# One encoder layer in fp32 on one core: the instructions are ordered on a simulated timeline instead of a plain machine model

## The chip, the cores and the metric

The kernel runs on one core of one Trainium2 chip. Its time is the device time of one execution in microseconds. Before the change it is 2390.23 us, the median of three runs that lie between 2390.2 and 2392.87 us.

The core has five engines that each work through their own list of instructions in the order in which the program holds them: PE (TensorE, matrix products and transposes), DVE (VectorE), ACT (ScalarE), POOL (GpSimd) and SP (SyncE, which here does nothing but start transfers). An instruction waits on semaphores for its inputs and for the buffer it writes, and everything behind it on the same engine waits too. Transfers are started by SP, ACT or POOL instructions and then run on their own.

## The reference

One layer on 1024 tokens of width 1024, batch 1, all in float32. The three sub-layers are normed before and after:

```python
f = swiglu(rmsnorm(h, pre1), w_gate1, w_up1, w_down1);   h = h + 0.5 * rmsnorm(f, post1)     # width 2816
z = rmsnorm(h, pre2) @ w_in                                                                   # 1024 -> 3456
y_att  = attention(z[:, :1536])    # 8 heads of 64, rotary; three dilated windows (128,1), (512,4), (2048,16),
                                   # mixed by their softmax denominators; each head normed
y_rwkv = rwkv7(z[:, 1536:])        # 8 heads of 64, token shift, forward and backward delta-rule scans, summed,
                                   # group norm, bonus, gate
mix = concat(y_att, y_rwkv) @ w_out;                     h = h + rmsnorm(mix, post2)
f = swiglu(rmsnorm(h, pre3), w_gate2, w_up2, w_down2);   out = h + 0.5 * rmsnorm(f, post3)
```

## The kernel before

**Products.** Every large product splits its fp32 operands into a high part that PE takes in one pass and the remainder (`split`: ACT copies the high part, line 186, DVE subtracts it, line 187), and sums three matmuls: high by high, high by low, low by high. The two feed-forward parts use a recursion with seven products in place of eight (lines 81 and 415).

**The run, in order.** First feed-forward part (to about 690 us in the profiled execution); low-rank projections and attention values; projection of queries and keys with rotation (`project_attention`: products `zq` line 440, transposes `zt` line 486, copy `zts` line 488, stores to DRAM `q_d` and `kt_d` line 489; then one stream of RWKV columns, `zs`, lines 306 to 309); attention; RWKV; the out projection; the second feed-forward part.

**Attention** (`attention`, line 739). For each of eight heads a "far" part (scores `s`, line 626, row maximum, exponential, transposes line 638, values line 644, a trip through DRAM) and a "near" part of eight query tiles (scores lines 685 and 686, masked maximum on DVE line 687, exponential on ACT line 691, transposes line 700, values line 707); line 732 is DVE's product that closes a head. The far part and the operand copies of the next head (lines 660 to 665) are issued inside the near part of this one.

**The RWKV projection** (`project_rwkv`). Eleven column blocks of 128 in six groups; each block takes 48 matmuls of 128x512 (`zr`, line 510, 528 in all), fed by loads `zraw` on SP and splits `zh`, `zl`. DVE then mixes neighbouring tokens into `us` (lines 524, 525). Value blocks are reversed (line 605) and transposed (`vt`, line 611, 64 transposes).

**The scan** runs in chunks of 64 tokens, two per block, eight blocks, both directions at once. For each block n, `prep` loads decays and keys (`th_w`, `th_a`, `in`; the last has one buffer), builds the scaled operands on DVE (lines 808 to 822), multiplies them on PE (line 830) and masks the result into `lm` (line 832, DVE, eight of them); the diagonal pieces of `lm` go to DRAM (`d_x`, line 846). `solve` loads them back as `X` (through `load`, line 182), and inverts on DVE in 31 dependent steps of two instructions each (lines 866 and 868), closing with line 870; the result goes to DRAM again (lines 872, 873). `merge` takes it from there (lines 883 to 900), and `chain` runs two dependent steps per block (xu, st, y: lines 937 to 952), each of which hands the state on through line 968 on DVE. `project_attended` (transposes `yq` 1075, products `po` 1064, fed by `yat` 1072 and `yal` 1078) puts the attention half of the out projection between them. `finish_unit` (f_y line 994 and f_k line 997 on POOL, line 999 on DVE) turns the scan's output into operands of the out projection.

**What sets the order.** The Python program emits every instruction once, in the order of its calls, and a scheduler then makes the list of each engine. It may put an instruction anywhere that its data allow. Its ties go by the order of emission, which `high_priority()` around one piece at the start raises, and `issue_after` in `_GateUp.rest` (line 162) holds four sums behind a given store. The scheduler advances a machine model as it places instructions; in this kernel it is the plain one, the default of the context that line 1431 opens. Buffers, their number and their place in memory come from the pools and are the same in both versions, as are all lines of code.

## Time and profile before

| | |
|---|---|
| time, median of 3 runs | 2390.23 us (2390.2 to 2392.87) |
| profiled execution: its own time | 2398.21 us |
| its span, first to last instruction | 2396.4 us |
| mean granted TensorE clock | 0.951 |
| PE busy | 2233.1 us, 93% of the span |
| DVE, ACT, POOL busy | 1778.9, 1030.6 and 572.8 us |

Times in the trace count from the start of the span. Where the stages lie there: first feed-forward part 0 to 690; projections 690 to 914; attention 918 to 1170 (its first scores start at 918.22, line 732 of the last head at 1169.4); RWKV preps, solves, merges and chain 1170 to 1624; out projection 1634 to 1740; second feed-forward part to the end. A row of a timeline gives start, duration, engine, line, operation, output and inputs, shape, and in brackets the idle time of the engine before it with what ended it. A matmul's duration is longer than its share of PE, since matmuls overlap: what a matmul costs is the distance from its start to that of the next.

### The profile page before, as it was taken

To read this page: it belongs to the slowest core of one execution; us is meant where nothing else is said; L and a number is where in the kernel's file an instruction comes from. 1 tells how busy PE (TensorE), PEld (TensorE's weight loads), DVE (VectorE), ACT (ScalarE), POOL (GpSimd) and SP (SyncE) were. 2 spreads that over 40 slices of the span, in tenths; PEclk is the share of its full clock that TensorE was granted. 3 is DMA by queue.
4 is the path that set the end of the run, shared out by engine and by line. 5 is a ranking of instruction groups with operands and counts; after the bars stand their busy time and mean duration, and the time that the engine had idled before them with its cause. 6 is when DMAs were issued, how large, how long until landed. Compare 5 with 4: busy or idle time off the path is not lost. (4 is left out here: it accounts for less than half of the span.)

```text
span 2396.4 us, 39330 instructions
## 1 busy us (share of the span) xinstructions
PE 2233.1 (93%) x14532; PEld 1801.5 (75%) x14532; DVE 1778.9 (74%) x2917; ACT 1030.6 (43%) x1918; POOL 572.8 (24%) x668
## 2 busy tenths in 40 slices
PE   6999999999999998999986788898989999999997
PEld 4788888788786676778775577775768888887886
DVE  8899999865675345666556766746889999997565
ACT  4422333354676304556544444445442233335452
POOL 6244344500000010111101121132234443442000
PEclk8999999999999998999995698789989999999999
DMA  5344544576743415322366766558534544448655
GB/s 155 110 172 150 171 158 156 181 257 194 227 152 133 161 50 157 84 71 72 91 173 174 177 157 166 146 173 268 186 107 172 180 150 167 164 152 268 194 189 180
DMA packets 359763, 386.03 MB, mean 161 GB/s; under 512 B 73618, under 2 KB 268050, under 8 KB 359572
## 3 DMA queue, kind: packets, MB, share of 16 engines
q1 hardware_dynamic: 311968, 284.82, 39.5%
q0 software_dynamic: 27248, 86.05, 9.7%
q10 hardware_dynamic: 20356, 12.66, 1.8%
q8 instruction: 114, 1.87, 0.3%
q14 instruction: 77, 0.63, 0.1%
HBM read 257.53 MB, written 125.89 MB: 160 GB/s over the span
## 5 line engine op out<-in xcount | busy, mean ns | idle before, releaser
L186 ACT ACTIVATE wh<-raw 128x512 fp32r<-128x512 f32 (+1 forms) x273 | 168.2, 627 | 261.8 <-DVE raw L62 94.0
L81 PE MATMUL gu<-xh,wh 128*128 128x512 f32 x704 | 277.2, 394 | 2.3 <-ACT wh L186 1.1
L187 DVE TENSOR_TENSOR wl<-raw,wh 128x512 fp32r<-128x512 f32 (+1 forms) x273 | 275.6, 1013 | 2.1 <-ACT wh L186 1.2
L81 PE MATMUL gu<-xh,wl 128*128 128x512 f32 x704 | 275.9, 392 | 0.0
L81 PE MATMUL gu<-xl,wh 128*128 128x512 f32 x704 | 275.7, 392 | 0.0
L415 PE MATMUL pd<-gl,gwh 128*128 128x512 f32 x616 | 240.5, 390 | 2.5 <-DVE gl L187 2.5
L415 PE MATMUL pd<-gh,gwh 128*128 128x512 f32 x616 | 239.6, 390 | 0.6 <-DVE row L86 0.6
L415 PE MATMUL pd<-gh,gwl 128*128 128x512 f32 x616 | 239.8, 389 | 0.0
L86 DVE TENSOR_TENSOR row<-gu,row 128x512 f32<-128x512 f32 x308 | 206.3, 682 | 26.1 <-PE gu L81 24.2
L187 DVE TENSOR_TENSOR gwl<-graw,gwh 128x512 fp32r<-128x512 f32 (+1 forms) x176 | 117.9, 672 | 128.4 <-ACT gwh L186 125.7
L116 POOL DMA_DIRECT2D d_hid<-row x154 | 84.7, 551 | 473.3 <-DVE row L114 446.2
L186 ACT ACTIVATE gwh<-graw 128x512 fp32r<-128x512 f32 (+1 forms) x176 | 101.4, 576 | 188.4 <-PE pd L415 157.5
L81 PEld LDWEIGHTS gu<-xh,wh 128*128 128x128 f32 x704 | 133.5, 190 | 31.6 <-ACT xh L186 2.0
L81 PEld LDWEIGHTS gu<-xl,wh 128*128 128x128 f32 x704 | 133.4, 189 | 27.5
L81 PEld LDWEIGHTS gu<-xh,wl 128*128 128x128 f32 x704 | 133.1, 189 | 27.6
L415 PEld LDWEIGHTS pd<-gl,gwh 128*128 128x128 f32 x616 | 115.6, 188 | 28.0 <-DVE gl L187 4.3
L415 PEld LDWEIGHTS pd<-gh,gwh 128*128 128x128 f32 x616 | 115.6, 188 | 25.3 <-DVE row L86 1.0
L415 PEld LDWEIGHTS pd<-gh,gwl 128*128 128x128 f32 x616 | 115.7, 188 | 23.8
L187 DVE TENSOR_TENSOR gl<-raw,gh 128x512 fp32r<-128x512 f32 x160 | 112.3, 713 | 17.0 <-ACT gh L186 16.7
L94 ACT ACTIVATE row<-row 128x512 f32<-128x512 f32 x44 | 27.8, 633 | 221.3 <-DVE row L86 217.5
L145 POOL TENSOR_TENSOR ws<-ws 128x512 f32<-128x512 f32 x88 | 114.2, 1298 | 1.1
L186 ACT ACTIVATE gh<-raw 128x512 fp32r<-128x512 f32 x160 | 98.0, 621 | 33.7 <-DMA raw<-in_ffn_w_down_dram 21.8
(354 smaller groups left out, 5345.7 us busy)
## 6 DMA issues: line engine op xcount, KB each, us to landing
d_hid<-row POOLq DMA_DIRECT2D x154, 256.0 KB, 2.4
graw<-d_hid SPq DMA_DIRECT2D x132, 256.0 KB, 3.0
raw<-in_ffn_w_gate_dram SPq DMA_DIRECT2D x88, 256.0 KB, 3.0
raw<-in_ffn_w_up_dram SPq DMA_DIRECT2D x88, 256.0 KB, 3.3
ws<-in_ffn_w_down_dram SPq DMA_DIRECT2D x88, 256.0 KB, 4.5
d_ws<-ws POOLq DMA_DIRECT2D x88, 256.0 KB, 2.3
raw<-d_ws SPq DMA_DIRECT2D x88, 256.0 KB, 2.7
raw<-in_ffn_w_down_dram SPq DMA_DIRECT2D x66, 256.0 KB, 3.6
```

The lines of the kernel that those rows point to most:

```text
L81: self.K.nc.tensor.matmul(ps, a[:, k, :], b[:, k, :], start=(k == 0 and i == 0), stop=(k == 3 and i == 2))
L86: add = lambda o, x: V.tensor_tensor(o, ps, x, op=OP.add)
L94: A.activation(y[:, 0], y[:, 0], AF.Silu)
L116: put = lambda n, y: G.dma_start(self.hid[n - 1, j // 2], y)
L145: G.tensor_tensor(o, a, b, op=OP.subtract)
L186: self.nc.scalar.activation(h, src, AF.Copy)
L187: (eng or self.nc.vector).tensor_tensor(l, src, h, op=OP.subtract)
L415: T.matmul(ps[x], a[:, ts], b, start=(m == 0 and k == 0), stop=(m == NM - 1 and k == 2))
```

## The change

```diff
-    with tile.TileContext(nc) as tc:
+    with tile.TileContext(nc, schedule_with_timeline_sim=True) as tc:
```

The scheduler now advances a simulated timeline in which every engine and every transfer queue has its own occupancy, and chooses the next instruction of an engine by it. Nothing else differs: both programs hold the same instructions, lines, tiles and buffers, and the same number on each engine. What differs is the order of each engine's list, and with it where waits stand.

On PE, rows 481 to 2900 and 9139 to the end of 11544 instructions, which are the bodies of the two feed-forward parts, stand in the same order; on DVE, ACT, POOL and SP neighbours there change places by one to four. Rows 3850 to 8200, which hold attention, the RWKV projection and the scan, move by up to 1412 places. Three places follow.

PE, the end of the projections and the start of attention. `zs` are the last matmuls of the projection, `zt` the transposes of rotated queries, `s` the far scores of head 0, `pt` its transposes, `zr` the RWKV projection. Before:

```order
L306 MATMUL zs<-xh_5434,wh 128x512
L307 MATMUL zs<-xl_5435,wh 128x512
L309 MATMUL zs<-xh_5432,wl 128x512
L309 MATMUL zs<-xh_5434,wl 128x512
L626 MATMUL s_7793<-kp,qp 64x64 x16
L510 MATMUL zr<-xh_5432,zh 128x512
L638 MATMUL pt_7817<-ident,sb_7811 128x128 x4
L510 MATMUL zr<-xl_5433,zh 128x512
L510 MATMUL zr<-xh_5434,zh 128x512
```

Now:

```order
L309 MATMUL zs<-xh_5432,wl 128x512
L309 MATMUL zs<-xh_5434,wl 128x512
L486 MATMUL zt<-ident,zo 128x128 x12
L626 MATMUL s_7793<-kp,qp 64x64 x16
L510 MATMUL zr<-xh_5432,zh 128x512
L510 MATMUL zr<-xl_5433,zh 128x512
L510 MATMUL zr<-xh_5434,zh 128x512
L510 MATMUL zr<-xl_5435,zh 128x512
L510 MATMUL zr<-xh_5432,zl 128x512
L510 MATMUL zr<-xh_5432,zh 128x512
```

The transposes of the last three query tiles, three times four, now stand behind all `zs`; before, the last of them stood among the `zs`. Behind the scores stood one `zr` matmul ahead of `pt`, now stand 15. Over the whole of attention, from the first `s` to the last `po` of line 707, the list now holds all 528 `zr` and all 64 `vt` in place of 238 `zr` and no `vt`: 133, 99, 83, 107, 101 and 5 `zr` in heads 0 to 5 and none in the last two.

PE, the end of attention (`po` of line 707 is the last head's product with the values). Before:

```order
L510 MATMUL zr<-xh_5434,zl 128x512
L510 MATMUL zr<-xh_5434,zh 128x512
L707 MATMUL po<-vn,e_10134 64x64 x6
L510 MATMUL zr<-xl_5435,zh 128x512
L510 MATMUL zr<-xh_5434,zl 128x512
L510 MATMUL zr<-xh_5432,zh 128x512
L510 MATMUL zr<-xl_5433,zh 128x512
```

Now (`yq` and `po` of line 1064 are the attended projection, `lp` is prep's product):

```order
L707 MATMUL po<-vn,e_10090 64x64 x10
L707 MATMUL po<-vn,e_10117 64x64 x8
L700 MATMUL pt_10135<-ident,sb 128x128 x3
L707 MATMUL po<-vn,e_10134 64x64 x6
L1075 MATMUL yq<-ident,yat 128x128 x4
L830 MATMUL lp<-pr,bk 128x128 x12
L1064 MATMUL po<-woh,yah 128x512
L1064 MATMUL po<-wol,yah 128x512
L1064 MATMUL po<-woh,yal 128x512
```

Before, 290 `zr` and the 64 `vt` followed; now the preps follow at once, and the attended projections stand between them.

DVE, the start of solve 3 (`X` is the piece of `lm` that comes back from DRAM, 128x31 the first step of a solve). Before, from the closing row of solve 2:

```order
L821 TENSOR_TENSOR th_a<-th_a,in_12997 128x512
L868 TENSOR_TENSOR Ti<-Ti,ttmp 128x3x15
L822 TENSOR_TENSOR bk<-th_a,th_w 128x8x64
L866 TENSOR_TENSOR ttmp<-X,Ti 128x30
L1078 TENSOR_TENSOR yal<-yq,yah 128x512
L868 TENSOR_TENSOR Ti<-Ti,ttmp 128x2x15
L866 TENSOR_TENSOR ttmp<-X,Ti 128x16
L868 TENSOR_TENSOR Ti<-Ti,ttmp 128x16
L870 COPY X<-Ti 128x512
L1072 TENSOR_TENSOR yat<-yat,rs 128x512
L866 TENSOR_TENSOR ttmp<-X,Ti 128x31
L868 TENSOR_TENSOR Ti<-Ti,ttmp 128x31
```

Its own prep's last `lm` stands 23 rows ahead of the first step. Now:

```order
L832 TENSOR_TENSOR lm<-lp,k_tri 128x512 x2
L815 SCALAR_TENSOR_TENSOR bk<-bk,th_w 128x8x64
L822 TENSOR_TENSOR bk<-th_a,th_w 128x8x64
L832 TENSOR_TENSOR lm<-lp,k_tri 128x512 x2
L814 SCALAR_TENSOR_TENSOR bk<-th_a,in_12997 128x8x64
L815 SCALAR_TENSOR_TENSOR bk<-bk,th_w 128x8x64
L821 TENSOR_TENSOR th_a<-th_a,in_12997 128x512
L822 TENSOR_TENSOR bk<-th_a,th_w 128x8x64
L832 TENSOR_TENSOR lm<-lp,k_tri 128x512 x4
L866 TENSOR_TENSOR ttmp<-X,Ti 128x31
L868 TENSOR_TENSOR Ti<-Ti,ttmp 128x31
L866 TENSOR_TENSOR ttmp<-X,Ti 128x30
```

The last four `lm` of prep 3 stand directly ahead of the first step of solve 3. The number of DVE rows between the last `lm` of a block and the first step of its solve was 8, 19, 38, 23, 7, 16, 37 and 29 for blocks 0 to 7, and is 11, 13, 63, 0, 0, 5, 13 and 9. Solves 0 and 1, which stood apart, now alternate step by step.

After the last head DVE's list loses seven pairs of lines 524 and 525, nine of line 187, four of line 605 and eight of line 1055, which now stand inside attention. At the end of the scan one pair of line 999 now stands ahead of the third last chain step's line 968 and two more pairs ahead of the second last; before, the first line 999 came behind the second last chain step. At the program's start, up to about 80 us, DVE's splits of the first weights stand ahead of splits of the input that stood before them.

## The prediction, made before the changed kernel was run

> **What bounds the kernel now.** I read the page's busy line and slices first, then busy time by stage.
>
> ```profile
> span 2396.4 us, 39330 instructions
> PE   6999999999999998999986788898989999999997
> DVE  8899999865675345666556766746889999997565
> ```
>
> PE is full in every slice of the two feed-forward parts (up to slice 11 and from slice 29). Their PE list is the same in both programs, so 80 to 690 us and most of what follows 1760 can move only through neighbours that change places on DVE. The gaps lie in slices 15 and 20 to 26, and stages show them:
>
> ```profile
> 80.00:690.00 610.00, 607.11 (x2692) 500.52 (x2691) 518.92 (x637) 239.51 (x428) 179.57 (x209) 1.00 0.55 182
> 918.00:1170.00 252.00, 243.16 (x2433) 194.54 (x2434) 170.94 (x488) 154.45 (x341) 31.79 (x31) 0.94 0.31 89
> 1170.00:1313.00 143.00, 117.08 (x856) 97.06 (x854) 77.97 (x157) 62.97 (x115) 19.13 (x32) 0.82 0.62 163
> 1313.00:1624.00 311.00, 264.04 (x4181) 214.05 (x4180) 205.73 (x621) 141.62 (x266) 62.05 (x92) 0.84 0.63 166
> ```
>
> The columns are busy PE, weight loads, DVE, ACT, POOL, then granted clock, DMA share and GB/s. In the first row PE is busy 607 of 610 us. In the last two neither PE nor DVE (206 of 311 us) is full: a chain of short steps sets the time there, prep on DVE, store and load of `X`, solve on DVE, merge, chain step. The end of that chain (1624 us) lets the rest of the program begin, so the time moves by as much as it moves. I therefore follow four dates: the first scores of attention, its last head, the last solve, the last chain step.
>
> **The start of attention: +11 us.**
>
> ```profile
> 902.65 0.39 PE L440 MATMUL zq<-z0l,xh 128*128 128x512 f32 x1
> 902.88 0.39 PE L440 MATMUL zq<-z0h,xl 128*128 128x512 f32 x1
> 906.15 0.63 PE L486 MATMUL zt<-ident,zo 128*128 128x128 f32 x4 [0.16 <-DVE zo L482]
> 906.81 0.69 DVE L488 COPY zts<-zt 128x512 f32<-128x512 f32 x1 [0.81 <-PE zt L486]
> 907.81 0.75 POOL L489 DMA_DIRECT2D d_q<-zts  x1 [5.19 <-DVE zts L488]
> 914.34 0.62 PE L309 MATMUL zs<-xh,wl 128*128 128x512 f32 x2
> 918.22 3.39 PE L626 MATMUL s<-kp,qp 64*64 64x64 f32 x32 [3.26 <-DMA kp<-d_kt]
> ```
>
> Two starts of 128x512 matmuls lie 0.23 us apart; that is their price. The last `zt` starts at 906.15, and 12.1 us later, after copy, store and load, the scores start. In the new list three groups of `zt` stand behind all `zs`, whose last start is at 914.34 + 0.23 us. The first of the three can run then; if DVE is up to date so can the last, and the scores come at about 927; if not, each of the three waits for three DVE products and a copy of 0.69 us (2.8 us), up to 8 us in all, and they come at 935. I take 929, because DVE's list brings these products forward: +11 (8 to 17).
>
> **Attention: +45 us.** The stage by heads, `zr` alone, and DVE's closing product:
>
> ```profile
> L732 DVE TENSOR_TENSOR ya<-po,c x8: 684/684/692, 968.1 to 1169.4; 128x512 f32<-128x512 f32 x8
> 918.22:968.06 49.84, 11.34 (x30) 0.83 0.44 136
> 968.06:1153.44 185.38, 65.96 (x202) 0.96 0.29 80
> 1169.42:1257.00 87.58, 70.79 (x290) 0.98 0.57 155
> ```
>
> Attention lasts 918.2 to 1169.4, 251 us, with 240 `zr` (30, 202 and 8). 290 follow, and all of them move in: 290 x 0.227 = 66 us of PE, and 64 `vt` at 0.63/4 = 0.16 or less, at most 10; I count 7. Were nothing of it hidden, attention would last 251 + 73 = 324. What can hide it: six heads take 185.4 us with 202 `zr` (46 us), so a head without them takes about 23 us; head 0 takes 49.8 with 30 (7 us), 20 us more than such a head, in which PE waits for loads and splits. Head 0 now has 133 `zr`, which can fill those 20. In heads 1 to 4 (83 to 107 each, 19 to 24 us) some 5 us a head of gaps can be filled, by the granted clock of 0.96 and by the 14 us that the bare last head takes. That gives 324 - 40 = 284 at best. But they stand in blocks of 15 to 24, and each of those (3.4 to 5.4 us) holds up whichever `pt` or score behind it is ready, and a block waits itself for its splits on ACT and DVE. I take two thirds filled, 296: +45 (33 to 73). The last head then ends at 929 + 296 = 1225.
>
> **After attention: less work and fewer waits, -59 us.**
>
> ```profile
> L524 DVE SCALAR_TENSOR_TENSOR us<-u,c_rwkv_mu_prev,us 128x1023 f32<-128x1023 f32 x7 | 9.2, 1313 | 14.5 <-ACT us L523 14.5
> L525 DVE SCALAR_TENSOR_TENSOR us<-u,c_rwkv_mu_next,us 128x1023 f32<-128x1023 f32 x7 | 9.0, 1279 | 0.0
> L1055 DVE SCALAR_TENSOR_TENSOR wol<-wor,c_attn_out_g,woh 128x512 fp32r<-128x512 f32 x8 | 6.0, 744 | 0.0
> L187 DVE TENSOR_TENSOR zl<-zraw,zh 128x256 fp32r<-128x256 f32 x9 | 3.6, 424 | 5.5 <-ACT zh L186 5.5
> L605 DVE COPY vrev<-us 128x1024 f32<-128x1024 f32 x4 | 2.7, 686 | 0.0
> DVE pr L810 <- DMA in<-d_rk: 17.8, 5, 8.3
> ```
>
> These groups of 1170 to 1624 move into attention: 9.2 + 9.0 + 6.0 + 3.6 + 2.7 = 30.5 us of DVE. With them go their waits, 14.5 + 5.5, and the 8.3 us for which the first prep waited on keys that the projection had only just stored: 28.3. In attention they cost DVE nothing on the path while it is busy 171 of 252 us; if that cover went, their 30.5 us would return. `zr` itself was PE work beside these.
>
> **The solves: +27 us.** This is the term that decides.
>
> ```profile
> 1227.47 3.75 SPq L846 DMA_DIRECT2D d_x<-lm  x4
> 1237.76 1.11 SPq L182 DMA_DIRECT2D X<-d_x  x2
> 1244.95 0.18 DVE L866 TENSOR_TENSOR ttmp<-X,Ti 128x31 f32<-128x31 f32 x1
> 1364.00:1379.90 15.90, 8.29 (x26) 0.68 0.85 211
> sum 144.40, DVE 87.78; mean DVE 10.97
> L870 DVE COPY X<-Ti x8: 582/598/623, 1267.5 to 1584.0; 128x512 f32<-128x512 f32 x8
> ```
>
> From the first store of `d_x` to the first step of its solve it takes 17.5 us for block 0, 15.9 for block 3, the shortest of the eight. Summed over the eight blocks (windows from each store to its solve's start, of which one row and the sum are shown) that is 144.4 us; DVE worked in 87.8 of them and stood for 56.6. In the new list the instructions that stand there are 11, 13, 63, 0, 0, 5, 13 and 9; by the durations of their groups they hold 6, 4, 15, 0, 0, 3, 3 and 2 us, 33 in all. DVE is in order, so nothing from further down can fill in. With windows of 15.9 us DVE would stand 8 x 15.9 - 33 = 94 us, 38 more than now. If the load of `X` followed its store with nothing between on SP, a window could shrink to 3.75 us of issue and the median landings of both, which the next rows give:
>
> ```profile
> d_x<-lm SPq DMA_DIRECT2D x32, 64.0 KB, 3.7
> X<-d_x SPq DMA_DIRECT2D x16, 256.0 KB, 5.1
> ```
>
> 12.6 us, and 101 - 33 = 68, 11 more than now. In the new list SP does issue `X` right behind `d_x` in most blocks, so I take windows of 14.5: 116 - 33 = 83, +27 (11 to 38). The Trainium skill (DMA: Bandwidth & Descriptors, "Anatomy of one DMA") gives a DMA of the GpSimd path about 2 us plus its bytes over 436 GB/s; two in a row would take some 5 us, and by that estimate the new order would leave DVE standing some 19 us and this term would be about -37. The 17.5 us above do not bear it out here.
>
> The last solve, now ending with the row at 1584.0, comes at 1584 + 11 + 45 - 59 + 27 = 1608.
>
> **The end of the chain: +2 us; the start: +1.**
>
> ```profile
> 1593.65 1.39 DVE L968 TENSOR_TENSOR sv<-st,gc 64x512 f32<-64x512 f32 x2 [5.83 <-PE st L937]
> 1606.64 0.88 DVE L999 SCALAR_TENSOR_TENSOR f_k<-f_k,rkc,f_r 128x256 f32<-128x256 f32 x2 [11.60 <-POOL f_k L997]
> 1615.45 1.41 DVE L968 TENSOR_TENSOR sv<-st,gc 64x512 f32<-64x512 f32 x2 [2.81 <-PE st L937]
> PE pt L330 <- DVE xl L187: 17.7, 6, 10.1
> ```
>
> Line 999 waits 11.6 us for POOL, which waits for loads of the scan's output. Today two chain steps stand ahead of it; in the new list it stands ahead of them, so they are queued behind that wait and PE's next step behind them. But the last step cannot come before merge 7, 31 us after the last solve (1584 to 1615), and that covers it unless the wait exceeds some 20 us: +2 (0 to 15). In the first 80 us PE waits 17.7 us for DVE's splits, the same number of splits in another order: +1 (0 to 5). Swaps of neighbours in the feed-forward bodies: 0, hidden by PE at 607 of 610 us.
>
> **The sum.** 11 + 45 - 59 + 27 + 2 + 1 = +27 us. The profiled execution took 2398.21 us, 1.8 more than its span and 8.0 more than the median of the runs; it would become 2425, and the median 2390.2 + 27 = 2417.
>
> **Rivals.**
>
> *Attention swallows the projection (faster, 2380).* The `zr` fill all 40 us of gaps (+33) and the start costs its least (+8), the `X` windows shrink to 12.6 (+11): 8 + 33 - 59 + 11 = -7, and -10 with an attention a little closer to full. For it: today's 252 us hold many short gaps. Against: the blocks, and two last heads with no filler. It decides where attention ends before about 1205. Chance 0.24.
>
> *Loads in SP's list hold up attention (slower, 2450).* SP now issues twenty `zraw` loads ahead of the far load of head 0, and later groups of four between the loads of the next heads; each waits for a buffer of four, and what stands behind it on SP waits too. From its load (issued 915.98 us) to its first use a block took 7.8 us; if each of the last five of seven groups stalls a head so, +39 on the sum, less what the gaps give: about 2450. For it: SP is in order. Against: groups of `zraw` stood among the same loads before, in other numbers. Chance 0.14.
>
> ```profile
> 915.98 2.22 SPq L182 DMA_DIRECT2D zraw<-in_w_in_dram  x4
> 923.82 0.80 PE L510 MATMUL zr<-xh,zh 128*128 128x512 f32 x1 [2.21 <-ACT zh L186]
> ```
>
> *It cancels (2390).* Less work after attention pays for the longer attention and the windows: attention at +35, windows at +11, the start at +8 give -3 to +3. For it: the PE work is the same in sum. Chance 0.12.
>
> **How the numbers follow.** Forecast 0.50, rivals 0.24, 0.14 and 0.12. A change under 0.2% (4.8 us) cannot be told from none here. Faster by more: 0.24; within: 0.12; slower: 0.64. The forecast's own range, from the ends of its terms taken half way, is 2400 to 2435. The range of 8 in 10 takes in the cancelling case, most of the faster one and about half of the slow one: 2373 to 2448.
>
> **What would show it.** Right: first scores near 929; last line 732 near 1225 with no `zr` after it; eight stretches from `d_x` to line 866 of 14 to 16 us in which DVE is busy 33 to 45 us together; waits of line 866 on `X` of 40 us or more, against little today; last line 870 near 1608, last line 968 near 1640; clock in the solve stage lower than 0.84. Wrong: the last head before 1205 or after 1245; the windows covered by other work; or a change in the feed-forward bodies, which I hold at nothing.

## The result, and the profile after

The changed kernel takes 2526.24 us (median of 4 runs, 2518.41 to 2537.8), the kernel before 2391.55 us in the same comparison (2390.2 to 2394.91): a ratio of 1.0565, 95% interval 1.0522 to 1.0608. The prediction had the sign, but 2417 us and a range that ends at 2448: the loss is 135 us, not 27. The new order's times also lie further apart.

The profiled execution is the fastest of the four: 2518.41 us, span 2516.3. The kernel before was profiled in an execution of 2398.21 us, so the spans differ by 119.9 us, less than the medians. These dates are starts of instructions in the two traces:

| us from the start of the span | before | after | difference |
|---|---|---|---|
| last `pd` of the first feed-forward part (415) | 690.9 | 699.5 | +8.6 |
| first scores of attention (626) | 918.2 | 936.2 | +18.0 |
| line 732, head 0 | 968.1 | 1010.3 | +42.3 |
| line 732, head 4 | 1095.6 | 1198.5 | +102.9 |
| line 732, head 7 | 1169.4 | 1281.8 | +112.4 |
| last `zr` (510) | 1256.6 | 1199.7 | -56.8 |
| last solve (870) | 1584.0 | 1681.8 | +97.8 |
| last chain step (968) | 1616.2 | 1726.7 | +110.5 |
| last `pd` of the second feed-forward part | 2381.6 | 2502.0 | +120.4 |

The page after, busy line and slices:

```profile
span 2516.3 us, 39323 instructions
PE   5999999999999969999867767778969999999997
DVE  6799999855763445655657654654788999997565
PEclk9999999999999989999878867678979999999999
```

The gaps on PE (slices counted from 0) were in 15, 20 to 25, 27 and 29 before and are now in 14, 19 to 27 and 29; the clock is now below 0.9 in slices 14, 19 to 27 and 29. By stages of the kernel after (columns as in the prediction: PE, weight loads, DVE, ACT, POOL busy, then granted clock):

```profile
936.20:1281.80 345.60, 326.29 (x2784) 264.82 (x2784) 203.45 (x520) 187.14 (x399) 33.59 (x39) 0.95 0.35 98
1010.30:1060.30 50.00, 49.08 (x405) 40.58 (x406) 31.22 (x80) 34.30 (x68) 5.49 (x7) 1.00 0.36 109
1149.50:1198.50 49.00, 49.00 (x400) 40.33 (x401) 25.55 (x61) 21.21 (x46) 4.39 (x5) 1.00 0.35 92
1198.50:1233.80 35.30, 31.44 (x305) 25.76 (x304) 24.17 (x61) 21.83 (x48) 5.71 (x6) 0.85 0.51 125
1233.80:1265.10 31.30, 23.01 (x230) 16.62 (x231) 18.14 (x61) 14.43 (x34) 2.22 (x2) 0.84 0.37 98
1281.80:1681.80 400.00, 287.88 (x3809) 241.31 (x3811) 247.49 (x724) 150.37 (x285) 58.80 (x98) 0.75 0.52 135
```

Attention takes 345.6 us in place of 251.2. Heads 1 and 4 (second and third row) hold 99 and 101 `zr` and fill PE (49.08 of 50.00 us and 49.00 of 49.00), at full clock. Heads 5 and 6 hold 5 and none (head 5 also 29 `vt`) and still take 35.3 and 31.3. The same view of the kernel before, heads 3 to 5, and the stretch from the last head to the last solve:

```profile
1029.60:1065.70 36.10, 36.10 (x329) 28.78 (x327) 23.25 (x68) 21.90 (x47) 5.26 (x5) 0.91 0.28 80
1065.70:1095.60 29.90, 29.89 (x309) 24.06 (x308) 20.52 (x58) 19.09 (x39) 3.65 (x4) 1.00 0.28 75
1095.60:1123.80 28.20, 28.20 (x302) 22.51 (x301) 21.48 (x64) 20.05 (x46) 3.91 (x5) 1.00 0.29 77
1169.40:1584.00 414.60, 345.55 (x4313) 282.65 (x4314) 274.27 (x758) 186.86 (x347) 65.85 (x107) 0.82 0.61 158
```

Heads 1 to 6 held 28 to 40 `zr` there and took 28 to 36 us; heads 5 and 6, with 28 and 34, took 28.2 and 29.6, less than now with 5 and none. In heads 3 to 5 PE stood for nothing. From the last head to the last solve 290 `zr` and 27 us of DVE work are gone (274.27 to 247.49), and the stretch is only 14.6 us shorter (414.6 to 400.0). What DVE waits for in it, in the kernel after (waits of 1282 to 1682; total, times, longest):

```profile
DVE ttmp L866 <- DMA X<-d_x: 34.3, 7, 8.9
DVE pr L810 <- DMA in<-d_rk: 23.6, 7, 5.4
DVE bk L814 <- DMA in<-d_rk: 21.6, 5, 7.0
DVE sv L968 <- PE st L937: 20.8, 3, 18.1
```

Line 968 hands the state from one chain step to the next. In the changed kernel it often comes late, although its input `st` is there (start, duration, operation):

```profile
1470.85 0.22 PE L937 MATMUL st<-uv,bt 128*64 128x64 f32 x1
1480.75 1.39 DVE L968 TENSOR_TENSOR sv<-st,gc 64x512 f32<-64x512 f32 x2
```

The product was done at 1471.1 us, and line 968 came 9.7 us later, behind rows of solve 3 and of a preparation in DVE's list. Summed over the 15 steps, line 968 starts 59.9 us after its `st` is done; before, it was 5.4 us. PE's next product waits for it accordingly, after (first row) and before (total, times):

```profile
  PE xu L941: 27.7, 9
  PE xu L941: 3.4, 3
```

So the chain falls behind the solves. The timeline after solve 4 of the kernel after (in brackets the engine's idle time and what ended it):

```profile
1526.98 0.61 DVE L870 COPY X<-Ti 128x512 f32<-128x512 f32 x1
1529.33 1.41 DVE L968 TENSOR_TENSOR sv<-st,gc 64x512 f32<-64x512 f32 x2 [1.74 <-PE st L937]
1548.86 1.41 DVE L968 TENSOR_TENSOR sv<-st,gc 64x512 f32<-64x512 f32 x2 [18.12 <-PE st L937]
1554.18 0.22 PE L937 MATMUL y<-pr,sv 64*64 64x64 f32 x1
1554.29 0.69 DVE L810 TENSOR_TENSOR pr<-in,e 128x512 f32<-128x512 f32 x1 [4.02 <-PE y L937]
...
1562.61 0.69 DVE L814 SCALAR_TENSOR_TENSOR bk<-th_a,in 128x512 f32<-128x512 f32 x1 [7.02 <-DMA in<-d_rk]
```

Between 1531 and 1562 DVE does almost nothing. The second line 968 waits 18.1 us, because its `st` stands in PE's list behind merge 4's products, which wait 5.0 us for merge 4's trip through DRAM. Line 810 of block 5 comes next and could not have come sooner: after line 968 it waits another 4.0 us for the chain's product `y`, which still reads the old `pr`. Blocks 3 and 5 share one buffer for it (`R0`, line 1286), in both kernels. Before, the chain was ahead of the solve:

```profile
1453.60 0.68 DVE L968 TENSOR_TENSOR sv<-st,gc 64x512 f32<-64x512 f32 x1
1459.98 0.60 DVE L870 COPY X<-Ti 128x512 f32<-128x512 f32 x1
1460.49 0.68 DVE L810 TENSOR_TENSOR pr<-in,e 128x512 f32<-128x512 f32 x1
```

These are the same step, the end of solve 4 and line 810 of block 5: it followed the solve by 0.5 us, and now by 27.3. So solve 5 comes 101 us after solve 4; before, it came 71 after.

After the last solve, in the kernel after:

```profile
1681.79 0.60 DVE L870 COPY X<-Ti 128x512 f32<-128x512 f32 x1
1694.76 0.31 PE L937 MATMUL st<-uv,bt 128*64 128x64 f32 x1
1698.42 2.91 DVE L999 SCALAR_TENSOR_TENSOR f_k<-f_k,rkc,f_r 128x256 f32<-128x256 f32 x2 [16.03 <-POOL f_k L997]
1701.36 0.68 DVE L968 TENSOR_TENSOR sv<-st,gc 64x512 f32<-64x512 f32 x1
```

Line 968 stands behind line 999, which waits 16 us. Its `st` was done at 1695.1, so this costs the step 6.3 us. The chain was late before that, too: the step ahead of it came 2.0 us before the last solve, where it had come 10.5 before.

### The profile page after: what moved, and what is told of

Its sections match the earlier page's. It is cut to its first block, busy times and chain, and to the rows that moved or that the text cites. A ratio compares the mean times of both kernels' runs of the same rounds, so it can differ in the third digit from the quotient of the medians.

```text
span 2516.3 us, 39323 instructions
## 1 busy us (share of the span) xinstructions
PE 2270.5 (90%) x14532; PEld 1845.2 (73%) x14532; DVE 1753.3 (70%) x2917; ACT 1026.0 (41%) x1918; POOL 569.3 (23%) x668
## 5 line engine op out<-in xcount | busy, mean ns | idle before, releaser
L187 DVE TENSOR_TENSOR wl<-raw,wh 128x512 fp32r<-128x512 f32 (+1 forms) x273 | 288.5, 1060 | 18.0 <-ACT wh L186 12.4
L186 ACT ACTIVATE wh<-raw 128x512 fp32r<-128x512 f32 (+1 forms) x273 | 162.5, 622 | 214.8 <-DVE raw L62 152.5
L86 DVE TENSOR_TENSOR row<-gu,row 128x512 f32<-128x512 f32 x308 | 206.0, 681 | 16.7 <-PE gu L81 14.1
L187 DVE TENSOR_TENSOR gwl<-graw,gwh 128x512 fp32r<-128x512 f32 (+1 forms) x176 | 112.3, 639 | 128.0 <-ACT gwh L186 125.2
L116 POOL DMA_DIRECT2D d_hid<-row x154 | 84.9, 552 | 462.9 <-DVE row L114 448.0
```

Of the source, the lines that this page charges most:

```text
L86: add = lambda o, x: V.tensor_tensor(o, ps, x, op=OP.add)
L116: put = lambda n, y: G.dma_start(self.hid[n - 1, j // 2], y)
L186: self.nc.scalar.activation(h, src, AF.Copy)
L187: (eng or self.nc.vector).tensor_tensor(l, src, h, op=OP.subtract)
```

## The experiments

**How a list is fixed.** Eleven kernels carry a table of instruction numbers (the same in both programs) and this helper. It adds edges between neighbours of the table that only order them in an engine's list and put no wait on the chip:

```diff
+def _pin(tc, nc):
+    found = {i.name: i for i in nc.cur_bb.bb.instructions}
+    link = mybir.DependencyInfo(mybir.DependencyClass.NoSync, mybir.DependencyReason.DATA)
+    for row in _PINS:
...
+        for p, q in zip(seq, seq[1:]):
+            tc.add_manual_dep(found[f"I-{q}"], f"I-{p}", link, reason="pin")
...
         _Kernel(tc, io, out).run()
+        _pin(tc, nc)
```

So parts of one program can run in the order of the other. What is not in a table or held back, the scheduler orders anew, and this can be a third order: by the traces DVE's scan list is that of the changed kernel, place for place, only where `zs` or the closing part is moved and where it is itself the table; it is that of before wherever it is in a table of old lists; in the other runs on the changed program, and where attention's new order is put into the kernel before, only 126 to 248 of its 710 places agree with the changed kernel.

Ratios are against the kernel before on the same chip (2391.5 to 2396.2 us), with 95% intervals. A difference of 10 to 15 us between two of the slow kernels is no more than their spread: the run with the closing part moved has the changed kernel's lists up to there, and its profiled execution ends attention 10 us later (1292.2).

### One suspected cause each

**The projection partly moved back.** 288 of the `zr`, and the `vt`, behind attention's last value product:

```diff
-            self.project_rwkv(zr, pz, x, [(4, 2), (6, 2), (1, 1), (2, 2)])
+            self.project_rwkv(zr, pz, x, [(4, 2), (6, 2), (1, 1)])
+            with self.tc.issue_after(self.po.ins):
+                self.project_rwkv(zr, pz, x, [(2, 2)])
             blk = {0: self.prep(0, sp, pp, R0)}
             self.solve(0, sp)
-            self.project_rwkv(zr, pz, x, [(8, 2), (10, 2)])
+            with self.tc.issue_after(self.po.ins):
+                self.project_rwkv(zr, pz, x, [(8, 2), (10, 2)])
```

> The new order with one part undone: the last 288 zr matmuls (the column groups from block 2, from 8 and from 10) and what follows them on TensorE are queued behind attention's last product, so that heads 2 to 7 hold almost none. In the profile of the change attention took 346 us (251 before) and paid back 15 us after it. Theory 1, the zr and vt in the heads lengthen attention by their whole price or more and the chain after attention does not get it back: the last head ends 70 to 95 us earlier than at 1282, the last solve 40 to 75 us earlier than at 1682, and the time falls by 40 to 75 us from the 2526 of the change. Theory 2, the matmuls cost the same wherever they stand, and the loss sits in the order of preps and solves: attention ends earlier by as much, but the last solve and the time stay within 15 us of the change.

2511.13 us, ratio 1.0487 (1.0445 to 1.0528). The last head comes 44 us earlier than in the changed kernel (1238.1), but last head to last solve takes 434 us, 34 more: 15 us are gained by the medians. Theory 2 by the last solve (10 us earlier) and, at its edge, by the time; but 288 `zr` (65 us) taken out bring the last head only 44 us forward, not as much. Its heads 4 to 6, which hold no `zr` (same view as above):

```profile
1129.90:1159.80 29.90, 26.00 (x265) 19.96 (x264) 17.83 (x54) 14.78 (x35) 3.26 (x3) 0.85 0.25 63
1159.80:1194.50 34.70, 29.39 (x263) 22.67 (x264) 17.90 (x54) 14.99 (x34) 3.29 (x3) 0.69 0.11 24
1194.50:1223.50 29.00, 26.47 (x236) 19.68 (x235) 14.38 (x52) 11.49 (x31) 3.42 (x4) 0.72 0.14 29
```

A bare head takes 29 to 35 us at a clock of 0.69 to 0.85. Heads 3 to 6 together, all without `zr`, take 127.9 us; before, with 134 `zr` and a clock of 0.91 to 1.00, they took 123.9. Those `zr` were free, and moving all out of a head saves nothing.

**The attended projection's weights out of attention.**

```diff
-            WA = self.out_weights(eo, 0, self.aog)
+            with self.tc.issue_after(self.c3.ins):
+                WA = self.out_weights(eo, 0, self.aog)
```

(`self.c3` is the last head's last exponential.)

> The new order with the splits of the output weights (wor, woh, wol) queued on ScalarE behind the last head's last small exponential, so that heads 5 to 7 are free of them. In the profile of the change these three heads took 83 us with 5 zr, against 74 us before with 79 zr. Theory 1, the serial load, ACT and DVE steps of the one wor buffer stand in front of attention's own ACT and DVE steps: the three heads take 60 to 68 us, the last head ends 15 to 23 us earlier, the time falls by 5 to 20 us (the eight splits, 6 us of DVE and 8 loads one after the other, come back behind it). Theory 2, the heads are slow because TensorE runs at a lower granted clock there with nothing to fill it (0.83 to 0.90): they stay within 5 us of 83 us and the time within 5 us.

2510.68 us, 1.0488 (1.0445 to 1.0531). The last three heads take 33.7, 30.3 and 15.9, 80 in place of 83: theory 2, the splits were not what slows them. Their clock is 0.85, 0.71 and 1.00. The time falls by 15.6 us, which theory 1 had; but attention ends 4 us later (1285.8), and what is gained comes behind it (last solve 1672.9), where the scan has a third order.

**The RWKV columns `zs` behind the last `zt`.**

```diff
+            with self.tc.issue_after(zt.ins):
+                self.product_into(ps, x, [(wh[:, k, :], wl[:, k, :]) for k in range(NK)], (0, 1))
```

> The new order with the 48 zs matmuls queued behind the last zt transposes. In the profile of the change the last zt start at 924.0 and the first far scores at 936.2, 18 us later than before. Theory 1, the late zt set the start of attention: the last zt come 8 to 12 us earlier, the first scores too, and the time falls by 7 to 12 us. Theory 2, head 0 is bound by its 133 zr, whose inputs do not hang on the zt: the first scores come earlier but head 0 ends within 4 us of 1010 and the time stays within 4 us.

2532.33 us, 1.0571 (1.0528 to 1.0615). The first scores come at 933.0, 3 us earlier than in the changed kernel, now right behind the last `zs` (932.6), and head 0 ends at 1016.1, 6 us later: nothing of it is left. Nearest theory 2, whose 4 us both head 0 and the time pass by 2. This test could gain 3 us at most.

**The closing part's products behind chain step 13.**

```diff
+            with self.tc.issue_after(self.step[13].ins):
+                self.finish_half(fi, pf, 0, x)
```

> The new order with DVE's part of the first half of the finish queued behind the state product of the third last chain step but one (line 968 of step 13), as it stands before the change. In the profile of the change the last line 968 comes 45 us after the last solve, before the change 32 us. Theory 1, line 999, which waits for POOL and for loads of the scan's output, holds up the last chain steps: the distance falls to 31 to 35 us and the time by 8 to 14 us. Theory 2, the last steps wait for merge 7 or for their own loads, and the finish merely fills: the distance stays over 41 us and the time within 4 us.

2537.86 us, 1.0605 (1.0569 to 1.0641): no faster. Theory 2 by the distance, while the time is 12 us longer, which neither had. From last solve to last line 968 it takes 49.0 us. In place of line 999, line 968 itself now waits (19.0 us for `st`, 10.4 for a transfer). To move that one piece on DVE is not enough.

### Lists of one or two engines

**DVE's scan list as before** (710 instructions, lines 808 to 870 and 968) in the changed kernel:

```diff
+_PINS = [
+    (
+        "10929 10931:10932 10934:10935 10941 10997 10942 10955:10956 10999 10967:10968 11000 11002:11003 11009:11010 "
...
```

> The new order, with one list pinned: VectorE's 710 instructions of preps, solves and chain (lines 808 to 832, 866 to 870 and 968) stand among themselves in the sequence they had before the change; the scheduler is free with all else, attention included. In the profile of the change the last solve comes 400 us after the last head (415 before, with the RWKV projection still in it), and for 18 us line 968 waits for TensorE while the next prep's instructions stand behind it. Theory 1, such waits of line 968 and of the solves ahead of work that could run are what the scan loses: the distance from the last head to the last solve falls to 345 to 375 us, and the time by 25 to 55 us against 2526. Theory 2, the round trips through DRAM set the scan whatever stands between them: the distance stays within 10 us of 400 and the time within 10 us.

2501.17 us, 1.0455 (1.0429 to 1.0481). Last head to last solve 375 us in place of 400, the end of the chain 42. The 25 us are theory 1's, at its lower end. Line 810 of block 5 comes 1.1 us after solve 4 in place of 27.3, and solve 5 comes 79 us after it in place of 101. But line 968 waits no less than in the changed kernel (22.8 us for `st` against 20.8), so its waits, which both theories start from, were not what was lost.

**PE's attention and `zr` list as before** (1952 instructions):

```diff
+_PINS = [
+    (
+        "7794:7809 10244 7818:7821 10245 10268 7825:7840 7865:7866 10246 7871:7886 7895:7896 10247:10250 7908 7902:7904 "
...
```

> The new order, with one list pinned: TensorE's 1952 instructions of attention and of the RWKV projection (lines 510, 587, 597, 611, 626, 638, 644, 685, 686, 700, 707) stand among themselves in the sequence they had before the change, so each head holds 10 to 40 zr and 290 follow attention. Theory 1, some 30 zr in each head cost nothing because they fill gaps and keep TensorE's clock up, 100 in a head cost their price, and heads without any run at a lower clock: attention takes 250 to 270 us instead of 346, the last head ends at 1185 to 1210, and since the scan then has the projection in it again (434 us from last head to last solve when 288 zr were held back in the run before) the time falls by 30 to 70 us against 2526. Theory 2, attention's own steps on VectorE and ScalarE, which this leaves in the new order, lengthen it: attention stays over 300 us and the time falls by less than 20.

2485.32 us, 1.038 (1.0348 to 1.0412). Attention shrinks to 275 us, not to 251; the front is new here, and DVE's and ACT's lists of attention are a third order. Last head to last solve grows to 429. 41 us gained: theory 1, with attention and the last head (1216.6) 5 to 7 us past its bounds.

**Both tables together.**

> Both pins at once: VectorE's scan instructions and TensorE's instructions of attention and projection in the sequence from before the change. Theory 1, these two lists hold nearly all of the loss: the last solve comes 405 to 425 us after the last head, attention takes 250 to 270 us, and the time is 2405 to 2430, which leaves about 18 us to the start of attention and 8 us to the second feed-forward part. Theory 2, the loss is spread over transfers and the other engines' lists: the time stays over 2450.

2472.29 us, 1.0335 (1.0311 to 1.0359): theory 2. 54 us gained, less than 25 + 41. 80 us are still lost, on the front, on the other engines of attention, in the scan (427) and in the chain's end (42).

**The reverse: the new DVE scan list alone, in the kernel before.**

```diff
+_PINS = [
+    (
+        "10929 10931:10932 10934:10935 10997 10941:10942 10999:11000 10955 11002 10956 11653 10967 11003 11009:11010 "
...
```

> The reverse: the kernel before the change with its own scheduler, but VectorE's 710 instructions of preps, solves and chain pinned among themselves to the sequence of the changed kernel. Theory 1, that sequence by itself costs what it saves in the pinned run of the change: the distance from the last head to the last solve grows from 415 to 435 to 465 us and the time by 15 to 50 us over 2391. Theory 2, the sequence is harmless unless attention is late: the time stays within 8 us.

2500.7 us, 1.0446 (1.042 to 1.0472). This one list, put where the projection is not yet done, costs 109 us, where theory 1 had at most 50: last head to last solve 513 us. Line 810 of block 5 comes 15 us after solve 4, and solve 5 comes 98 us after it. DVE's waits there:

```profile
DVE ttmp L866 <- DMA X<-d_x: 32.0, 4, 15.6
DVE pr L810 <- DMA in<-d_rk: 31.5, 7, 9.5
```

A list is made for the dates at which its inputs come. Laid over other dates, each wait holds what is behind it.

### Whole stages, all five engines

**The front as before** (all that is emitted ahead of attention):

> The new order, with the lists of all five engines pinned to the sequence from before the change for everything that the program emits ahead of attention (first feed-forward part, low-rank parts, projection of queries and keys). In the profile of the change the first far scores come 18 us later than before. Theory 1, these 18 us go into the time whole: the first far scores come at 915 to 922, the last head 14 to 22 us earlier than at 1282, the time falls by 12 to 25 us against 2526. Theory 2, attention is bound by the zr in head 0, whose inputs were there in time anyway, and swallows it (as when the zs alone were held back): the last head and the time change by less than 6 us.

2514.55 us, 1.0506 (1.0479 to 1.0533). The first scores come at 921.1, 15 us earlier than in the changed kernel, head 0 ends 10 earlier, and the last head at 1280.3, 1.5 earlier. Attention swallows the gain, at a clock of 0.92 to 0.97 in heads 1 to 4 where the changed kernel has 1.00. Why just so much is left open. Theory 2 by the last head; the time is 12 us shorter, between the two theories and within the spread.

**The front, attention and the RWKV projection as before; the scan and all behind it ordered by the timeline.**

> The new order, with the lists of all five engines pinned to the sequence from before the change for everything up to the end of attention and for the whole RWKV projection; only preps, solves, merges, chain, finish and the second feed-forward part stand in the new order. Theory 1, the scan's new order loses by itself: the last head ends at 1167 to 1177 as before the change, the last solve 425 to 445 us after it (415 before the change), and with 10 us each at the end of the chain and in the second feed-forward part the time is 2420 to 2455. Theory 2, the scan loses only because attention ends late: the time is within 12 us of 2391.

2450.42 us, 1.0236 (1.0217 to 1.0255): theory 1. The last head is back at 1174.1; last head to last solve takes 450 us, against 415 before and 445 as theory 1's most. So the scan loses by itself, though in an order that is not the changed kernel's.

**Preparations, solves, merges, chain and attended projection as before; all else new.**

> The new order, with the lists of all five engines pinned to the sequence from before the change for preps, solves, merges, chain and attended projection (with VectorE alone pinned the last solve came 375 us after the last head, and the last line 968 42 us after it; the time was 2501). Theory 1, what is left of the scan's loss lies in the lists of the other engines, above all in SP's and POOL's transfers: 350 to 368 us to the last solve, 31 to 36 us from there to the last line 968, time 2470 to 2490. Theory 2, VectorE's list was all of it: within 6 us of 375, of 42 and of 2501.

2484.66 us, 1.0377 (1.0353 to 1.0402): theory 1 by the time and the solves. Last head 1281.8, as in the changed kernel, and 366 us from there to the last solve in place of 400. The chain's end stays at 44, where theory 1 had 31 to 36.

**Everything behind attention as before, the closing part and the second network too.**

> The changed kernel, in which all five engines' lists for everything behind attention (preparations, solves, merges, chain, attended projection, closing part and second feed-forward network) go in the order of before; the front and attention keep the new order. Theory 1: the slower end of the chain (44 us from the last solve to the last line 968, against 32) and the 9 us at the start of the second feed-forward network come from where the closing part's loads and products stand among the last merges and steps in the lists. Then last solve to last line 968 takes 31 to 36 us, the second network adds 0 to 3 us, last head to last solve stays at 350 to 372, and the time is 2458 to 2476. Theory 2: they come with the late attention, whatever the order: 41 to 46 us, and 2478 to 2492.

2462.93 us, 1.029 (1.0262 to 1.0318): theory 1. Last solve to last line 968 is 33.9 us, and the second network adds nothing more. Its stretch from last head to last solve, and DVE's end of it:

```profile
1276.90:1643.10 366.20, 260.78 (x3959) 216.23 (x3960) 251.54 (x731) 158.69 (x296) 60.37 (x100) 0.78 0.60 154
```

```profile
1643.14 0.61 DVE L870 COPY X<-Ti 128x512 f32<-128x512 f32 x1
1645.63 1.41 DVE L968 TENSOR_TENSOR sv<-st,gc 64x512 f32<-64x512 f32 x2 [1.88 <-PE st L937]
1652.87 1.39 DVE L968 TENSOR_TENSOR sv<-st,gc 64x512 f32<-64x512 f32 x2 [5.83 <-PE st L937]
1665.30 0.88 DVE L999 SCALAR_TENSOR_TENSOR f_k<-f_k,rkc,f_r 128x256 f32<-128x256 f32 x2 [11.04 <-POOL f_k L997]
...
1676.32 1.41 DVE L968 TENSOR_TENSOR sv<-st,gc 64x512 f32<-64x512 f32 x2 [0.75 <-PE st L937]
```

Line 999 still waits 11 us for POOL, but two chain steps are ahead of it. Line 810 of block 5 comes 0.5 us after solve 4 again, and solve 5 71.5 us after it.

**All lists of the three parts as before, in the changed kernel.**

> The changed kernel with all five engines' lists in the order of before over the whole program, each of the three parts (front, attention with the RWKV projection, all the rest) in its own lists. Theory 1: the order within these parts is all that the change does: last head near 1174, last solve 1590 to 1605, and 2391 to 2410, so that what the parts cost one by one (76 and 42 to 60) adds up to the whole loss. Theory 2: something else is changed (which queue carries a transfer, which of two buffers a tile gets, how the three parts lie among each other): over 2415, with the place to be read from the dates.

2396.95 us, 1.0006 (0.999 to 1.0022): theory 1. The order within the lists is all of the loss. It also shows the spread of the stretches: 405.7 us from last head to last solve, where the profiled execution of the kernel before has 414.6. Its heads and solves:

```profile
L732 DVE TENSOR_TENSOR ya<-po,c x8: 685/686/692, 967.9 to 1169.1; 128x512 f32<-128x512 f32 x8
L870 DVE COPY X<-Ti x8: 589/598/605, 1266.4 to 1574.8; 128x512 f32<-128x512 f32 x8
```

**The reverse: attention and the projection in the new order, in the kernel before.**

```diff
+_PINS = [
+    (
+        "7794:7809 10244:10245 10268:10269 10246:10248 10270:10272 10249:10251 10273:10274 7818:7821 10275 10252:10254 "
...
```

> The kernel before, in which all five engines' lists for attention and the RWKV projection are in the new order; the front and everything behind attention keep theirs. Theory 1 (beyond some 30 a head, each zr costs its whole price, and heads left without any run at a lower clock): attention 320 to 346 us instead of 251, last head to last solve 365 to 400 instead of 414, so that the whole loses 20 to 55: 2412 to 2450. Theory 2 (the loss in attention comes from the late and disordered front, and the lists themselves fill gaps as the prediction had it): attention 285 to 310, and 2375 to 2405.

2445.54 us, 1.0197 (1.0165 to 1.0229): theory 1, with attention 2 us above its bounds and the stretch behind it 9 us below. The two:

```profile
921.60:1269.90 348.30, 329.49 (x2784) 267.79 (x2784) 203.00 (x520) 186.43 (x398) 34.12 (x40) 0.93 0.34 97
1269.90:1625.50 355.60, 267.51 (x3644) 218.98 (x3645) 246.35 (x724) 147.82 (x277) 58.81 (x98) 0.76 0.59 148
```

With an undisturbed front attention still takes 348 us, 97 more than before; the emptied stretch behind it, whose scan has a third order, takes 355.6, 59 less than 414.6.

### The short way of `X` alone

In the kernel before, SP's scan list with each load of `X` right behind its stores:

```diff
+_PINS = [
+    (
+        "11280 11650 11057:11060 11062:11063 11349:11350 11358:11359 11367:11368 11667 11376:11377 11714 11494:11495 "
...
```

> The kernel before the change with its own scheduler; SP's list of the scan (193 transfers) is pinned to its own sequence with one difference: the two loads of X stand directly behind their block's stores of d_x, ahead of the loads and stores that stood between. In the profile of the change, where they stand so in most blocks, the step from the last lm to the solve took 9 us, before the change 15 to 22. Theory 1, SP's list lengthens these steps before the change: they shrink to 8 to 12 us, VectorE stands 20 to 35 us less in them, and the time falls by 8 to 30 us against 2391. Theory 2, what stood between is needed as soon, and the wait moves to line 810 and line 832: the steps shrink but the time stays within 5 us or grows.

2399.84 us, 1.0017 (1.0000 to 1.0035): no gain. The windows from a block's last `lm` to its solve shrink from 129.5 to 109.6 us in sum, and DVE's standing in them from 54 to 44, but the last solve comes only 6 us earlier (1578.3), and with all lists as before it came at 1574.8 in another execution. DVE's rows changed places, too (404 of 710 as before), so this is not SP's list alone. Theory 2. None of the runs here beats the kernel before.

## Why the prediction was right in sign and wrong in size

The terms, as predicted and as the spans of the two profiled executions have them:

| step | predicted | measured |
|---|---|---|
| program start and start of attention | +1 + 11 | +18.0 |
| attention | +45 (33 to 73) | +94.4 |
| after attention: less work, and solves | -59 + 27 = -32 | -14.6 |
| end of the chain | +2 (0 to 15) | +12.7 |
| from there to the end (second feed-forward part) | 0 | +9.9 |
| sum | +27 | +120 |

The third row is good to some 9 us: with all lists as before, 405.7 us stood where the kernel before's profiled execution has 414.6.

**Attention: the step that failed.** Half the error (49 of 93 us) is here, and it is not the front's doing, since the new lists alone give 348 us in the old program. Two sentences of the step fell. "A head without them takes about 23 us" came from subtracting the `zr` price from heads that were full. 23.0 is indeed what PE *works* in head 6, but the head takes 31.3, because scores, maximum, exponential and transposes wait for each other, at a lower clock. The 28 to 40 `zr` that a head held before lay in just those gaps. And "some 5 us a head of gaps can be filled" fell because the gaps were filled already: PE was busy 28.20 of 28.20 us. The granted clock of 0.96 was read as a sign of gaps; head 3 had 0.91 with PE busy 36.10 of 36.10 us. A row by head would have shown that there were none.

So the last 290 `zr` cost their whole price, as in the step's own bound (324 = 251 + 73), and heads 5 and 6 came on top: 35.3 + 31.3 us where the step's 23 each make 46, +20. 324 + 20 is 344; measured 345.6. Counted by heads: heads 0 to 4 hold 354 `zr` more (80 us at 0.227) and 35 of the `vt`, and take 84.9 us more; heads 5 to 7 hold 65 fewer and take 9.4 us more.

**After attention: the work was nearly right.** The cleanest measure is the run with everything behind attention as before, whose scan lists are the old ones: the stretch falls from 414.6 us to 366.2, by 48 (by 40 from the 405.7 above), where the term had 59. With attention's new order in the kernel before it falls by 59, but there the scan has a third order; that this is the term to the us is luck.

**The solves: a fair size for the wrong reason.** 400.0 against 366.2 makes +34, in the term's range (11 to 38). But the windows did not stand open as the term had it. Two of them, of blocks 2 and 3, and the sum over the eight, in the kernel after:

```profile
1375.75:1400.34 24.59, 17.20 (x184) 12.89 (x184) 15.96 (x65) 8.73 (x15) 11.01 (x17) 0.93 0.68 169
1447.76:1456.70 8.94, 6.27 (x128) 5.74 (x126) 0.00 (x1) 2.90 (x6) 0.00 (x0) 0.80 0.66 139
sum 88.42, PE 75.06 PEld 61.83 DVE 36.39 ACT 32.36 POOL 16.80; mean PE 9.38 PEld 7.73 DVE 4.55 ACT 4.05 POOL 2.10
```

and the sum before:

```profile
sum 129.56, PE 112.98 PEld 93.73 DVE 75.42 ACT 68.51 POOL 12.84; mean PE 14.12 PEld 11.72 DVE 9.43 ACT 8.56 POOL 1.60
```

These windows run from the last `lm` to the solve's first step. DVE is busy 36.4 us in them (predicted 33 to 45), and stands 88.4 - 36.4 = 52.0 us, against 54.1 before. Counted from the first store, as the term did, it stands 57.0 us against 54.9, and block 3 takes 10.3 us, below the 12.6 that I took as the least. So the term's mechanism is worth -2 to +2, not +27. (Its base was misread a little: the windows of blocks 2, 4 and 6 began 2 to 4 us before their first store. From the stores the sum before is 135.8 us and the shortest window 14.8, block 4's.) The wait of line 866 for `X` did grow as forecast, from 7.4 to 34.3 us; before, DVE stood in the windows for other things.

What costs the 34 us stands between solves 4 and 5: 101 us there against 71 before, and 71.5 with the old lists behind attention; all the rest of the stretch differs by 4. There block 5's preparation waits for a chain that is late, because line 968 stands behind ready work of solves and preparations on DVE. DVE's list alone, put back, takes 25 of the 34 away, 22 of them between these two solves. That the shared buffer carries the wait is read from the rows and the code; no run gave block 5 a buffer of its own. With the old lists behind attention, DVE waits for the same things (waits of 1277 to 1643):

```profile
DVE pr L810 <- DMA in<-d_rk: 11.9, 4, 6.6
DVE ttmp L866 <- DMA X<-d_x: 10.1, 3, 3.7
DVE sv L968 <- PE st L937: 7.7, 7, 2.6
DVE bk L814 <- DMA in<-d_rk: 1.0, 2, 0.7
```

DVE stands 152.5 us of the 400.0 in the changed kernel and 114.7 of 366.2 here, 38 more, of which the windows are 6 (52.0 against 46.3). Line 968's own wait is 13 more; the waits for `in`, which has one buffer and comes back late when a preparation is held up, are 32 more, and others are shorter.

**The chain's end: the mechanism right, the value taken at the wrong end of the bound.** The step named what happened, line 968 behind line 999's wait, and held it covered by merge 7 "unless the wait exceeds some 20 us". A wait of 16.0 us was enough: it cost the step 6.3 us, and the chain came 8.5 us late into the last solve, which the step had left out. Moving the closing part's lists back gives 33.9 us in place of 44; moving its DVE piece alone gives nothing.

**The start.** First scores at 936 in place of 929: the `zt` behind the `zs` did wait for DVE (the bad end of the bound, 935). The first network ends 8.6 us later where +1 was taken, but the last `zs` comes only 0.8 us later (915.4 against 914.6), so that delay was made up. And the start's price was counted wrongly: of 15 us regained there, 1.5 arrive at the last head.

**The feed-forward bodies at nothing.** PE's list is the same, and yet the second network takes 9 to 10 us more. With the lists of before behind attention this goes to zero (60.9 us of delay at the chain's end, 59.0 at the end of the program). "Hidden by PE at 607 of 610 us" holds for the body, not for its beginning: from the 64th to the 160th product of line 81 PE takes 36.7 us in place of 26.0, and its longest waits around there are for DVE (4.6 us for line 266, 2.7 and 1.9 for splits of line 187).

**The rivals.** The slow one (SP's `zraw` loads hold up attention) had the better total, 2450, for a reason that does not show: in heads 1 to 4 PE is full. The others are out. What the profile was to show came true in part: no `zr` after attention, and a lower clock behind it (0.75 against 0.82). The last head at 1281.8 passes the 1245 that I had named as proof of the contrary.

Three runs differ from each other in whole stages with all five engines' lists fixed, and their steps make up the 135 us: the front and attention cost 66.7 us over the kernel before, the scan's five lists 45 more, and the closing part and the second network 23.

## What to carry to other kernels

Before filler work is moved into a stage, take that stage's windows unit by unit and look for PE's idle time in each: where the filler that is there already keeps it full, more of it costs its whole price, and the units that lose it do not get shorter by as much. Where each engine works through its list in order, look in a new list for the links of a chain of dependent steps, and ask what stands ahead of each when its input is ready, and which later work waits for that chain, through a shared buffer too; that placing, not the number of instructions, was worth 25 us here on DVE. To find where an order loses, fix the lists of one stage at a time to the old sequence and confirm with all of them fixed; a list that is left free can come out in a third order, so compare the lists before comparing the times.

## What was not expected of the hardware

PE's granted clock falls in heads whose longest wait is short. The longest wait on PE in the kernel after, 1198.5 to 1281.8:

```profile
PE pt L700 <- ACT sb L691: 2.8, 2, 2.5
```

No wait is longer than 2.5 us, and yet the clock is 0.84 to 0.90 there. The Trainium skill (TensorE: Matmul & The Clock Gate, "HAM oscillation — how this bites in real kernels") gives the rule that PE must have no idle gaps over about 3.4 us. Here gaps below that went with a lower clock: keeping under the rule was not enough. Full heads mostly had more, 0.91 to 1.00 with the 28 to 40 `zr` of the kernel before. But idle time is not all of it: head 3 there had 0.91 with no idle time on PE at all. What lowered it there stays open.

The trip of `X` through DRAM is short or long by more than SP's list tells. From the last `lm` to the first use it took 14 to 19 us in the kernel before and 7.2 to 9.2 in six of the eight blocks of the changed kernel. With the loads put right behind the stores in the kernel before it took 9.2 to 16.7. What else lengthens it there was not tried. The Trainium skill's estimate that the prediction gave (DMA: Bandwidth & Descriptors, "Anatomy of one DMA": some 5 us for two transfers in a row, by a figure for the GpSimd path, where these go through SP) is below every one of these.
